# An encoder layer in split fp32 on one core: first stage's order, one running sum P1 + P6, operands a pair ahead, and the order at the norm, the stage change and the end

## The chip, the core and the metric

The kernel runs on one core of a Trainium2 chip. The core has a matrix engine (TensorE, in the profile PE, with its weight loads as PEld), a vector engine (VectorE, DVE), a scalar engine (ScalarE, ACT), a general engine (GpSimd, POOL), and a queue for DMA issues (SyncE, SP). Each engine takes its instructions in program order, and semaphores order them across engines. The metric is the device time of one execution in microseconds; the time of a kernel is the median over its runs.

## The reference

One layer of a streaming encoder over 1024 prompt frames and 32 frames of a running stream (1056 columns here), width 1024:

```
h   = rmsnorm(x)
P   = h @ w_in                    # GLU, q, k, v, gates: 10240 columns
A   = pointwise(swish(layernorm(depthwise_conv31(GLU(P)))))
B   = (swish(gate) * groupnorm(retention(q, k, v))) @ w_ret_out    # 4 heads, chunks
x   = x + (sigmoid(g_conv) * A + sigmoid(g_ret) * B) @ w_out
x   = x + relu(rmsnorm(x) @ w_mlp1)^2 @ w_mlp2                     # 1024 -> 4096 -> 1024
y   = rmsnorm(x)
```

The outputs are y for both streams and the new convolution and retention states. All inputs and outputs are float32.

## The kernel before

Features lie on the 128 partitions and frames in the free dimension. An operand of a matmul is split in two fp32r parts, a high one (a cast, mostly on ACT) and a low one (the rest, a subtraction on DVE or POOL). A product is three matmuls per slice of 128 inputs: high by high, high by low, low by high.

**First stage.** The products with `w_in`, `w_ro`, `w_co` and `w_o` are a list of jobs, one per 128 output features. `run` takes them in order: each job has three chunks of 352 frames, and `group` issues the 24 matmuls of one chunk (8 slices by 3) into one PSUM bank. `load` and `split` fetch a job's weight and split it ahead of use (`whi` on ACT; `wlo` on POOL, or DVE where `j.eng` says so, L110). Side work is written as Python generators: `run` advances each of `sides` by one step after every group, and those in `mids` also in the middle of a group. So the order on the engines is fixed by the program, with the steps of the side work dealt out over the groups: the first norm (`norm1`), the convolution's taps on DVE (`conv_side`, L374, 31 taps per channel tile), and a retention head (`retention`), whose step has the values transposed and split (`vtlo`, L425), the scores (`att`, `atlo`), the output `po` with its statistics, and the transposition back (`pto`, L500). `gated0` splits the gated retention output for the product with `w_ro`.

**First MLP product.** It is done in a Strassen manner, with seven products of sums of blocks instead of eight, by a table that gives for each step the functions to call (`at`, `c0`, `c1`, ...). `early` and `ss` are buffers for hidden units; L1092 copies one PSUM bank out into `early`. Hidden units are squared on ACT and spilled to memory (`usp`).

**Second MLP product.** Four groups of hidden units, each with seven products P1 to P7 in the order 1, 2, 6, 7, 4, 5, 3. A unit is half of such a product's weights, fourteen per group, and has four products of 12 matmuls of 264 columns. P2, P4 and P3 accumulate on the banks of P1, P7 and P5, so the earlier one's bank is read out (`evac`) before the later one starts on it. P1 + P6 is kept in `acc`, a part of the buffer `yy`, and is added to two or more blocks of the result `R` (`add_a`, L1260, on POOL, each time 128 x 528). `last_pair` loads the first two operands and weights of this stage during the last products of the first MLP product: both operands go through `yy`, the weights A11 into `raw` and A12 into `early`. All loads are issued on SP, in the program's order.

**End.** In the last group, squares of the finished rows are summed in `ss` (`sq_half`, `sq`); `begin(q)` makes the statistics of a quarter (`st_fn`, then the power on POOL), `spread(q)` broadcasts them (`bc_fn`), `out_row` scales a row and `store` writes it. The last unit is four products of quarters.

Of the kernel before, what the change touches and what calls it, by code (L numbers as in the profile page):

```python
# [10 lines left out]
ALU = mybir.AluOpType  # L11
# [48 lines left out]
def encoder_step(ctx: ExitStack, tc: tile.TileContext, xT, par_d, idn_d, cst_d, rot_d, w_in, w_co, w_ro,  # L60
# [63 lines left out]
    room = {}  # L124
# [16 lines left out]
    def group(n, c):  # L141
        j = jobs[n]
        xh, xl = (a[c] for a in j.rhs())
        ps = room.pop((n, c), None)
        if ps is None:
            ps = bank(f"ps{n}_{c}", xh.shape[-1])
        for k in range(KT):
            if k == KT // 2:
                advance(mids)
            for m, (a, x) in enumerate(((j.hi, xh), (j.hi, xl), (j.lo, xh))):  # L150
                nc.tensor.matmul(ps, lhsT=a[:, k, :], rhs=x[:, k, :],  # L151
                                 start=(k == 0 and m == 0), stop=(k == KT - 1 and m == 2))
# [13 lines left out]
    def run(count, order=None):  # L166

        n0 = pos[0]
        order = order or [(i, c) for i in range(count) for c in range(NCH)]
        left = [sum(i == j for j, _ in order) for i in range(count)]  # L170
        low = None
        for i, c in order:
            now = n0 + next(q for q in range(count) if left[q])
            if now != low:
                low = now
                load(low)
                split(low)
                load(low + 1)
                load(low + 2)
                split(low + 1)  # L180
            group(n0 + i, c)
            left[i] -= 1
            advance(sides)
        pos[0] = n0 + count
# [72 lines left out]
    with tc.manual_schedule():  # L257
        xv = xT.rearrange("k p t -> p k t")
        with ExitStack() as ph:
# [307 lines left out]
            def norm1():  # L567
                r0 = stat(0, enter(0))
                yield
                q = enter(1)  # L570
                yield
                yield
                next(r0)
                yield
                yield
                r1 = stat(1, q)
                scale(0, r0)
                turn(0)
                yield
                q = enter(2)  # L580
                yield
                yield
                next(r1)
                yield
# [34 lines left out]
            sides.append(conv_side())  # L619
# [3 lines left out]
            for h in range(H):  # L623
# [9 lines left out]
                sides.append(r)  # L633
# [12 lines left out]
            def gated0():  # L646
                for _ in range(4):
                    yield
                for c in range(NCH):
                    for p in range(2):  # L650
                        g0[p].append(actA.tile([P, KT, CW], F32R, tag=("hi", "lo")[p] + str(c), name=f"g0_{p}{c}"))
                    for k in range(0, KT, 2):
                        ks = slice(k, k + 2)
                        split_act(g0[0][c][:, ks, :], g0[1][c][:, ks, :], g0raw[:, ks, cs[c]])
                        if c == 0:
                            yield
                    yield
                    if c == 1:
                        yield
# [190 lines left out]
        def product(ps, w, x, fresh=True):  # L850

            for k in range(QW):
                for m, (a, b) in enumerate(((w[0], x[0]), (w[0], x[1]), (w[1], x[0]))):
# [28 lines left out]
        s1w = yy[:, 2 * KT * P:2 * KT * P + QW * P].rearrange("p (k f) -> p k f", k=QW)  # L882
# [85 lines left out]
        def mlp1(cc):  # L968
# [73 lines left out]
            def c19():  # L1042
                nc.scalar.copy(xop["T3"][0], blk[1, 2])
                nc.scalar.copy(wop["S4"][0], raws[1][0][:, QW:])

            def c21():
# [3 lines left out]
            def c23():  # L1050
                low("T4", blk[2, 1])
                prep_op(1, "A22")

            def c24():
                U = place(0)
                for i, src in enumerate((early[:, 0], ss[:, hs[0]], ss[:, hs[1]], early[:, 1])):
                    nc.scalar.activation(out=U[:, i], in_=src, func=AF.Square)

            for i, fn in ((0, c0), (1, c1), (2, c2), (5, c5), (8, c8),
                          (9, lambda: nc.scalar.copy(xop["T1"][0], blk[1, 1])), (10, c10), (14, c14),  # L1060
                          (15, lambda: prep_a(2)), (17, c17), (19, c19), (20, c24), (21, c21),
                          (23, c23), (24, lambda: sums(0, place(0))), (26, lambda: prep_s(2, 1)),
# [134 lines left out]
        def last_pair(e):  # L1197

            at(e - 3, lambda: load_xs(0, kpieces(yy)))

            def a():
                for hf in range(2):
                    load_quad(wp, "raw", 2, 0, "A11", hf)
                for hf in range(2):
# [3 lines left out]
            at(e, a)  # L1208
            for k in range(4):
                at(e + 2 + k, lambda k=k: cut_x(0, k))  # L1210
                at(e + 10 + k, lambda k=k: cut_x(1, k))
            at(e + 5, lambda: load_xs(1, kpieces(yy)))
# [7 lines left out]
        def mlp2(cd):  # L1220
# [37 lines left out]
            def add_a(f, i, half):  # L1258
                r = R[:, f, hs[half]]
                nc.gpsimd.tensor_tensor(out=r, in0=r, in1=acc[:, i, :], op=ALU.add)  # L1260

            def evac(g, p, i, ps):
                final = g == NG - 1
                if p == 1:
                    nc.scalar.copy(fold(acc[:, i, :]), two(ps))
                elif p == 2:
                    add(i, 0, ps)
                elif p == 6:
                    tt(out=fold(acc[:, i, :]), in0=two(ps), in1=fold(acc[:, i, :]), op=ALU.add)  # L1269
                    if final:  # L1270
                        add_a(i, i, 1)
                elif p == 7:
                    add(i + 4, 1, ps)
                elif p == 4:
                    add(i + 4, 0, ps)
                    if final:
                        add_a(i + 4, i, 0)
                        add_a(i + 4, i, 1)
                    else:
                        add_a(i, i, 1)  # L1280
                elif p == 5:
                    add(i + 4, 1, ps)
                else:
                    add(i, 1, ps)
                    if not final:
# [26 lines left out]
            def begin(q):  # L1312
                rs[q] = rstd_bc(ss[:, qs[q]], pn, ("pn", "pn"), ss[:, qs[q]], RMS_EPS, f"fn{q}")
# [80 lines left out]
            for gi, (i, s) in enumerate([(2, 0), (3, 0), (2, 1), (3, 1)]):  # L1394
                ps = banks[5, i][:, s, :ST]
                w = [a[:, 4 * (i % 2):4 * (i % 2) + 4] for a in units[nu - 1]]
                product(ps, w, x_of(len(xj) - 1, s), False)
                if gi == 0:
                    sq_half(7, 1, False)
                elif gi == 2:  # L1400
                    begin(2)
# [7 lines left out]
                elif gi == 2:  # L1409
                    spread(2)  # L1410
                    for f in PRE1:
                        out_row(f, qs[2], None, True)
                    store(4, 7, qs[2])

            for f in (7, 0):
                out_row(f, qs[2], bcs[2])
            begin(3)
# [142 lines left out]
```

## Time and profile before

| | |
|---|---|
| runs | 2236.2 us median of 3 (2234.68 to 2237.6) |
| profiled execution | 2240.53 us, its span 2238.8 us |
| mean granted clock of TensorE | 0.99 |
| busy: PE / DVE / POOL / ACT | 2172.7 / 1487.8 / 846.4 / 682.0 us |
| matmuls | 14850 |
| first stage, by the trace | 0 to about 1530 us |
| first MLP product | about 1530 to 1867 us |
| second MLP product and end | about 1867 to 2238.8 us |

In the rows of the profile a time is in us unless ns is said; `out<-in` names the tiles by the program's names, `x4` is a count, and `[0.88 <-DVE vtlo L425]` behind a row is the time that the engine stood idle before it and what released it. A row of waits has the total, the number and the longest. A row of windows has, for one stretch, its length, the busy time and count of PE, PEld, DVE, ACT and POOL, the granted clock of TensorE, the busy share of the DMA engines and GB/s. A row of the chain of waits has the start, the length and what the chain went through.

### The profile page before, as it was taken

The page shows a single profiled execution, that of the slowest core. Times are in us where ns is not written, and L with a number is a line of the kernel's source. Part 1 is how long each engine was busy: PE and PEld are TensorE (multiplying, and loading weights), DVE is VectorE, ACT ScalarE, POOL GpSimd, SP SyncE. Part 2 cuts the span into 40 slices and gives each one's busy share as a digit, 9 for nine tenths or more (in the row PEclk, how much of TensorE's full clock was granted, in tenths as well). Part 3 has the DMA queues.
Part 4 walks back from the last instruction along what each step waited for, and adds up shares of the span by engine and source line. Part 5 has one row for each costly group of instructions (what it writes and reads, how often), then busy time and mean ns, then how long its engine had stood idle before and what let it go on. Part 6 is the DMA issues. An engine that isn't in the chain of part 4 may idle for free.

```text
span 2238.8 us, 35237 instructions
## 1 busy us (share of the span) xinstructions
PE 2172.7 (97%) x14850; PEld 2125.3 (95%) x14850; DVE 1487.8 (66%) x1936; ACT 682.0 (30%) x1056; POOL 846.4 (38%) x553
## 2 busy tenths in 40 slices
PE   7999999999999999999999999999899999999996
PEld 6999999999999999999999999999899999999996
DVE  7948886178861889538753674458555446887886
ACT  4113211132111321113243232234443444343342
POOL 4635555355553566525520353101222222311324
PEclk9999999999999999999999999999999999999997
DMA  4112131111221113111442333342344438633422
GB/s 167 48 49 68 39 106 67 38 59 48 105 67 39 63 44 112 51 49 58 154 142 96 112 103 106 130 154 90 139 169 173 154 118 306 230 130 123 173 76 78
DMA packets 93679, 237.00 MB, mean 106 GB/s; under 512 B 11473, under 2 KB 30161, under 8 KB 89937
## 3 DMA queue, kind: packets, MB, share of 16 engines
q1 hardware_dynamic: 93520, 234.75, 30.3%
q8 instruction: 116, 1.90, 0.3%
q14 instruction: 43, 0.34, 0.0%
HBM read 165.40 MB, written 69.32 MB: 105 GB/s over the span
## 4 chain that ended last, share of the span: by engine, by line
PE 80%; DVE 12%; issue 3%; ACT 1%; DMA 1%; POOL 1%; SPq 0%; POOLq 0%; DVEq 0%; ACTq 0%
PE ps L151 47%; PE m L854 13%; PE d L854 12%; DVE yc L374 4%; PE po L406 3%; PE pkv L406 2%; DVE xB_lo L859 1%; DVE o L315 1%; PE pto L500 1%; DVE h_lo L224 1%; DMA raw<-w_in 1%; DVE ss L808 1%; POOL wlo L110 1%; DVE R L926 1%; PE pt L422 1%
## 5 line engine op out<-in xcount | busy, mean ns | idle before, releaser
L151 PE MATMUL ps<-h_hi,whi 128*128 128x352 f32 x1904 | 621.4, 326 | 9.5 <-ACT h_hi L223 7.9
L151 PE MATMUL ps<-h_hi,wlo 128*128 128x352 f32 x1904 | 616.2, 324 | 4.5 <-POOL wlo L110 3.8
L151 PE MATMUL ps<-h_lo,whi 128*128 128x352 f32 x1904 | 614.1, 323 | 1.1 <-DVE h_lo L224 1.1
L374 DVE SCALAR_TENSOR_TENSOR yc<-glu,par,yc 128x1086 f32<-128x1086 f32 x240 | 421.2, 1755 | 3.4
L151 PEld LDWEIGHTS ps<-h_hi,whi 128*128 128x128 f32 x1904 | 359.1, 189 | 13.4 <-ACT h_hi L223 7.9
L151 PEld LDWEIGHTS ps<-h_hi,wlo 128*128 128x128 f32 x1904 | 359.9, 189 | 6.5 <-POOL wlo L110 5.5
L151 PEld LDWEIGHTS ps<-h_lo,whi 128*128 128x128 f32 x1904 | 360.6, 189 | 4.0 <-DVE h_lo L224 2.6
L110 POOL TENSOR_TENSOR wlo<-raw,whi 128x1024 fp32r<-128x1024 f32 x80 | 232.2, 2903 | 192.6 <-ACT whi L109 192.6
L854 PE MATMUL d<-xB_hi,v_hi 128*128 128x264 f32 x840 | 241.0, 287 | 10.0 <-ACT yy L807 4.4
L854 PE MATMUL d<-xB_hi,v_lo 128*128 128x264 f32 x840 | 239.9, 286 | 0.8 <-DVE v_lo L859 0.8
L854 PE MATMUL d<-xB_lo,v_hi 128*128 128x264 f32 x840 | 239.6, 285 | 0.0
L109 ACT CAST whi<-raw 128x1024 fp32r<-128x1024 f32 x120 | 125.5, 1045 | 342.7 <-PE ps L151 235.1
L854 PEld LDWEIGHTS d<-xB_hi,v_hi 128*128 128x128 f32 x840 | 159.1, 189 | 11.2 <-ACT yy L807 4.6
L1260 POOL TENSOR_TENSOR R<-R,yy 128x528 f32<-128x528 f32 x48 | 78.0, 1642 | 222.4 <-DVE yy L1269 105.8
L854 PEld LDWEIGHTS d<-xB_hi,v_lo 128*128 128x128 f32 x840 | 159.3, 190 | 1.4 <-DVE v_lo L859 1.4
L854 PEld LDWEIGHTS d<-xB_lo,v_hi 128*128 128x128 f32 x840 | 159.3, 190 | 0.0
L991 POOL TENSOR_TENSOR R<-R 128x1056 f32<-128x1056 f32 x16 | 39.4, 2463 | 254.2 <-ACT R L1150 200.2
L1140 DVE TENSOR_TENSOR R<-m,R 128x528 f32<-128x528 f32 x73 | 51.6, 707 | 124.3 <-PE m L854 124.3
L293 DVE TENSOR_TENSOR qkv<-ps,rms 128x352 f32<-128x352 f32 x48 | 25.1, 523 | 129.0 <-PE ps L151 129.0
L312 POOL TENSOR_TENSOR gsig<-gsig,o 128x352 f32<-128x352 f32 x48 | 74.5, 1553 | 82.5 <-ACT gsig L311 82.5
L151 PE MATMUL ps<-g,whi 128*128 128x352 f32 x384 | 92.0, 323 | 2.5 <-DVE gsig L310 2.5
L151 PE MATMUL ps<-z,whi 128*128 128x352 f32 x384 | 91.5, 321 | 0.0
(288 smaller groups left out, 4948.5 us busy)
## 6 DMA issues: line engine op xcount, KB each, us to landing
raw<-w_in SPq DMA_DIRECT2D x80, 512.0 KB, 4.0
usp<-R SPq DMA_DIRECT2D x16, 2112.0 KB, 7.4
xs<-usp SPq DMA_DIRECT2D x26, 1056.0 KB, 5.0
A<-w SPq DMA_DIRECT2D x30, 512.0 KB, 6.9
gate<-gt SPq DMA_DIRECT2D x16, 528.0 KB, 3.0
gsp<-o SPq DMA_DIRECT2D x16, 528.0 KB, 3.0
raw<-w_ro SPq DMA_DIRECT2D x16, 512.0 KB, 3.8
raw<-w_o SPq DMA_DIRECT2D x16, 512.0 KB, 3.6
```

The costliest lines, as they stand in the source:

```text
L109: nc.scalar.copy(j.hi, j.raw)
L110: j.eng.tensor_tensor(out=j.lo, in0=j.raw, in1=j.hi.bitcast(F32), op=ALU.subtract)
L151: nc.tensor.matmul(ps, lhsT=a[:, k, :], rhs=x[:, k, :], start=(k == 0 and m == 0), stop=(k == KT - 1 and m == 2))
L224: nc.vector.scalar_tensor_tensor(out=lo, in0=src, scalar=pcol(gcol), in1=hi.bitcast(F32), op0=ALU.mult, op1=ALU.subtract)
L293: nc.vector.tensor_tensor(out=late["qkv"][:, 4 + e, cs[c]], in0=ps, in1=rms[:, cs[c]], op=ALU.mult)
L312: nc.gpsimd.tensor_tensor(out=t, in0=t, in1=o[:, e, cs[c]], op=ALU.mult)
L374: nc.vector.scalar_tensor_tensor(out=y, in0=glu[:, t:t + YL], scalar=w, in1=y, op0=ALU.mult, op1=ALU.add)
L406: nc.tensor.matmul(out, lhsT=w, rhs=x, start=start and i == 0, stop=stop and i == 2)
L854: nc.tensor.matmul(ps, lhsT=a[:, k, :], rhs=b[k], start=(fresh and k == 0 and m == 0), stop=(k == QW - 1 and m == 2), skip_group_check=not ...
L991: gt(out=U[:, 4:6], in0=U[:, 1:3], in1=U[:, 0:2], op=ALU.subtract)
L1140: tt(out=fold(u[i]), in0=two(ps), in1=fold(x), op=ALU.add)
L1260: nc.gpsimd.tensor_tensor(out=r, in0=r, in1=acc[:, i, :], op=ALU.add)
```

## The change

- **Weight order**: `group` issues, for the first chunk of each weight but the very first, all products with the high half before those with the low half (8 x 2, then 8).
- **Taps**: `conv_side` becomes two generators, each with at most one tap per step. One stands ahead of the retention head in `sides`, the other behind.
- **First norm**: the steps of `norm1` are dealt out in another order (third chunk's split sooner, first broadcast later).
- **gated0**: the second chunk's splits are dealt out two and two.
- **First MLP product**: the squares of the first hidden units (`square0`) and some splits stand at other steps.
- **Stage change**: both first operands are loaded twelve steps ahead, one into `yy` and one into `early`; A12 goes into `early` nine steps later than before.
- **P1 + P6**: `acc` is summed over all four groups, and added to `R` in the last group alone, now on DVE. P1 of groups 1 to 3 is added from PSUM on DVE, where ACT copied it.
- **End**: the statistics of the third quarter are issued in the middle of the last product, their broadcast behind it, and the POOL rows behind that.

```
-        for k in range(KT):
-            if k == KT // 2:
+        todo = [(k, m) for k in range(KT) for m in range(3)]
+        if n and c in (0, first_of.get(n, 0)):
+            todo.sort(key=lambda t: t[1] == 2)
+        for i, (k, m) in enumerate(todo):
+            if i == len(todo) // 2:
                 advance(mids)
...
-            def conv_side():
+            def conv_side(every):
...
-                    for _ in range(2 if n % 3 else 1):
-                        if conv_ops:
-                            conv_ops.pop(0)()
+                    if conv_ops and (every or n % 3):
+                        conv_ops.pop(0)()
...
-            sides.append(conv_side())
+            taps2 = conv_side(False)
+            sides.extend([conv_side(True), taps2])
...
-                sides.append(r)
+                sides.insert(sides.index(taps2), r)
...
-                    yield
-                    if c == 1:
+                        elif c == 1 and k == 2:
+
+                            yield
+                            yield
+                    if c == 0:
                         yield
...
-            at(e - 3, lambda: load_xs(0, kpieces(yy)))
+            def first():
+                load_xs(0, kpieces(yy))
+                load_xs(1, kpieces(late["early"]))
+            at(e - 12, first)
...
-                at(e + 10 + k, lambda k=k: cut_x(1, k))
-            at(e + 5, lambda: load_xs(1, kpieces(yy)))
+                at(e + 6 + k, lambda k=k: cut_x(1, k))
...
+            at(e + 9, a12)
...
-                nc.gpsimd.tensor_tensor(out=r, in0=r, in1=acc[:, i, :], op=ALU.add)
+                tt(out=r, in0=r, in1=acc[:, i, :], op=ALU.add)
...
-                if p == 1:
+                if p == 1 and g == 0:
                     nc.scalar.copy(fold(acc[:, i, :]), two(ps))
-                elif p == 2:
-                    add(i, 0, ps)
-                elif p == 6:
+                elif p in (1, 6):
                     tt(out=fold(acc[:, i, :]), in0=two(ps), in1=fold(acc[:, i, :]), op=ALU.add)
...
-                product(ps, w, x_of(len(xj) - 1, s), False)
+                product(ps, w, x_of(len(xj) - 1, s), False, (lambda: begin(2)) if gi == 3 else None)
...
-                elif gi == 2:
-                    begin(2)
+                elif gi == 3:
+                    spread(2)
...
-            for f in (7, 0):
-                out_row(f, qs[2], bcs[2])
-            begin(3)
+            for f in PRE1:
+                out_row(f, qs[2], None, True)
+            store(4, 7, qs[2])
+
+            begin(3, True)
+            for f in (7, 0):
+                out_row(f, qs[2], bcs[2])
+            next(rs[3])
```

What the change does to the order shows at three places. The first is DVE in a retention step of the first head: `gt` is an evacuation of a gate, `yc<-glu` a tap, `vtlo` the split of the transposed values, `att` and `atlo` the scores. Before (line numbers are each kernel's own, so 374 before is 380 now):

```order
L393 TENSOR_TENSOR gt_1553<-ps_1_1591,rms 128x352
L374 SCALAR_TENSOR_TENSOR yc_1489<-glu_1376,par,yc_1489 128x1086 x2
L425 TENSOR_TENSOR vtlo<-pt,vthi 128x512
L435 SCALAR_TENSOR_TENSOR ktlo<-pk,cst,kthi 128x256
L438 TENSOR_TENSOR att<-pk,cst 128x128
L442 TENSOR_TENSOR atlo<-att,athi 128x128
L393 TENSOR_TENSOR gt_1553<-ps_2_1650,rms 128x352
```

Now:

```order
L399 TENSOR_TENSOR gt_1553<-ps_1_1591,rms 128x352
L380 SCALAR_TENSOR_TENSOR yc_1489<-glu_1376,par,yc_1489 128x1086
L431 TENSOR_TENSOR vtlo<-pt,vthi 128x512
L441 SCALAR_TENSOR_TENSOR ktlo<-pk,cst,kthi 128x256
L444 TENSOR_TENSOR att<-pk,cst 128x128
L448 TENSOR_TENSOR atlo<-att,athi 128x128
L380 SCALAR_TENSOR_TENSOR yc_1489<-glu_1376,par,yc_1489 128x1086
L399 TENSOR_TENSOR gt_1553<-ps_2_1650,rms 128x352
```

Of the two taps ahead of `vtlo` one stands behind `atlo` now, ahead of the next evacuation.

The second place is ACT in the first MLP product, where a bank is copied out into `early`. `xT_hi` and `xB_hi` are casts for products that come later, `R<-early` and `R<-ss` the squares of the first hidden units. Before:

```order
L1070 ACTIVATE ss<-m_14303 128x528
L1043 CAST xT_hi<-R 128x2112
L1044 CAST xB_hi<-raw_13930 128x512
L1057 ACTIVATE R<-early 128x528
L1057 ACTIVATE R<-ss 128x528 x2
L1057 ACTIVATE R<-early 128x528
L1092 COPY early<-m_14358 128x528
```

Now:

```order
L1080 ACTIVATE ss<-m_14303 128x528
L1102 COPY early<-m_14357 128x528
L1058 ACTIVATE R<-early 128x528
L1062 CAST xT_hi<-R 128x2112
L1058 ACTIVATE R<-ss 128x528 x2
L1064 CAST xB_hi<-raw_13930 128x512
```

The copy stands right behind the relu into `ss`; both casts and three of the squares follow it, and the first square stands ahead of these rows.

The third place is DVE in the last group of the second MLP product, at the evacuation of P4 (`R<-d`). `xB_lo` and `v_lo` are splits of the next operand and weights, `ss<-ss,yy` sums squares, and `R<-R,yy` is the sum P1 + P6 added to a block. Before:

```order
L1256 TENSOR_TENSOR R<-d_0_20461,R 128x528
L859 TENSOR_TENSOR xB_lo<-xs,xB_hi 128x528 x2
L808 TENSOR_TENSOR ss<-ss,yy 128x528
L1256 TENSOR_TENSOR R<-d_1_20493,R 128x528
L859 TENSOR_TENSOR xB_lo<-xs,xB_hi 128x528
L859 TENSOR_TENSOR v_lo<-A_31_19890,v_hi 128x1024
```

Now:

```order
L1271 TENSOR_TENSOR R<-d_0_20425,R 128x528
L1275 TENSOR_TENSOR R<-R,yy 128x528 x2
L871 TENSOR_TENSOR xB_lo<-xs,xB_hi 128x528 x2
L818 TENSOR_TENSOR ss<-ss,yy 128x528
L1271 TENSOR_TENSOR R<-d_1_20457,R 128x528
L1275 TENSOR_TENSOR R<-R,yy 128x528 x2
L871 TENSOR_TENSOR xB_lo<-xs,xB_hi 128x528
L871 TENSOR_TENSOR v_lo<-A_31_19862,v_hi 128x1024
```

Two adds of the sum follow each such evacuation on DVE; before, POOL had all of them, 48 in the four groups.

More of the change, by code (lines that the diff above doesn't have):

```diff
@@ L123, in encoder_step @@
     held, deferred, normed = [], [], [0]
-    room = {}
+    room, first_of = {}, {}
     rings = [(pm, "pm")]
@@ L146, in group @@
             ps = bank(f"ps{n}_{c}", xh.shape[-1])
-        for k in range(KT):
-            if k == KT // 2:
+        kinds = [(j.hi, xh), (j.hi, xl), (j.lo, xh)]
+        todo = [(k, m) for k in range(KT) for m in range(3)]
[3 more added lines that the diff above has]
+            if i == len(todo) // 2:
                 advance(mids)
-            for m, (a, x) in enumerate(((j.hi, xh), (j.hi, xl), (j.lo, xh))):
-                nc.tensor.matmul(ps, lhsT=a[:, k, :], rhs=x[:, k, :],
-                                 start=(k == 0 and m == 0), stop=(k == KT - 1 and m == 2))
+            a, x = kinds[m]
+            nc.tensor.matmul(ps, lhsT=a[:, k, :], rhs=x[:, k, :], start=(i == 0), stop=(i == len(todo) - 1))
         old = len(deferred)
@@ L169, in run @@
         order = order or [(i, c) for i in range(count) for c in range(NCH)]
+        for i, c in reversed(order):
+            first_of[n0 + i] = c
         left = [sum(i == j for j, _ in order) for i in range(count)]
@@ L576, in norm1 @@
                 r1 = stat(1, q)
-                scale(0, r0)
-                turn(0)
                 yield
@@ L581, in norm1 @@
                 yield
+                scale(0, r0)
                 yield
                 next(r1)
+                turn(0)
                 yield
@@ L848, in tick, with product @@
             step[0] += 1
-        def product(ps, w, x, fresh=True):
+        def product(ps, w, x, fresh=True, mid=None):
             for k in range(QW):
+                if mid and k == QW // 2:
+                    mid()
                 for m, (a, b) in enumerate(((w[0], x[0]), (w[0], x[1]), (w[1], x[0]))):
@@ L1040, in c17, with square0, c22 @@
                 nc.scalar.copy(xop["T4"][0], blk[2, 1])
-            def c19():
+            def square0(*rows):
+                U = place(0)
+                src = (early[:, 0], ss[:, hs[0]], ss[:, hs[1]], early[:, 1])
+                for i in rows:
+                    nc.scalar.activation(out=U[:, i], in_=src[i], func=AF.Square)
+            def c22():
+                square0(3)
                 nc.scalar.copy(xop["T3"][0], blk[1, 2])
+                square0(1, 2)
                 nc.scalar.copy(wop["S4"][0], raws[1][0][:, QW:])
-            def c21():
                 low("T3", blk[1, 2])
                 tt(out=wop["S4"][1], in0=raws[1][0][:, QW:], in1=wop["S4"][0].bitcast(F32), op=ALU.subtract)
[L1050 to L1057, printed above, removed]
             for i, fn in ((0, c0), (1, c1), (2, c2), (5, c5), (8, c8),
                           (9, lambda: nc.scalar.copy(xop["T1"][0], blk[1, 1])), (10, c10), (14, c14),
-                          (15, lambda: prep_a(2)), (17, c17), (19, c19), (20, c24), (21, c21),
-                          (23, c23), (24, lambda: sums(0, place(0))), (26, lambda: prep_s(2, 1)),
+                          (15, lambda: prep_a(2)), (16, lambda: square0(0)), (17, c17),
+                          (20, lambda: low("T4", blk[2, 1])), (22, c22), (23, lambda: prep_op(1, "A22")), (24, lambda: sums(0, place(0))), (26, lambda: prep_s(2, 1)),
                           (26, lambda: prep_s(2, 3)), (27, lambda: prep_s(2, 2)), (28, lambda: prep_op(2, "S2")),
@@ L1203, in a, with a12 @@
                     load_quad(wp, "raw", 2, 0, "A11", hf)
+            at(e, a)
+            for k in range(4):
+                at(e + 2 + k, lambda k=k: cut_x(0, k))
+                at(e + 6 + k, lambda k=k: cut_x(1, k))
+            def a12():
                 for hf in range(2):
```

35 lines of the change are left out of this document (9 added, 26 removed).

## The prediction, made before the changed kernel was run

> **What bounds the kernel now.** I read the page first (busy times, then groups), then the waits of TensorE, then the granted clock in short windows around the longest waits, and last the rows of the engine that each wait names.
>
> ```profile
> PE 2172.7 (97%) x14850; PEld 2125.3 (95%) x14850; DVE 1487.8 (66%) x1936; ACT 682.0 (30%) x1056; POOL 846.4 (38%) x553
> L1260 POOL TENSOR_TENSOR R<-R,yy 128x528 f32<-128x528 f32 x48 | 78.0, 1642 | 222.4 <-DVE yy L1269 105.8
> ...
> PE pto L500 <- DVE vtlo L425: 8.1, 8, 1.2
> PE m L854 <- ACT early L1092: 6.3, 2, 5.6
> PE bc_n L218 <- DVE rms L214: 4.5, 3, 2.7
> PE d L854 <- ACT yy L807: 4.4, 1, 4.4
> PE ps L151 <- POOL wlo L110: 3.8, 6, 0.7
> PE d L854 <- DVE R L1140: 2.9, 1, 2.9
> PE ps L151 <- DVE wlo L110: 2.6, 3, 1.0
> PE ps L151 <- DVE gsig L310: 2.5, 1, 2.5
> ```
>
> TensorE is the bound: 2172.7 of 2238.8 us busy. The change leaves its number of matmuls as it is, so it can save only idle time (66.1 us in all) and matmuls that ran at a low clock. The waits (total, times, longest) say which idle time. The low clock shows in these windows (length; busy time and count of PE, PEld, DVE, ACT, POOL; granted clock):
>
> ```profile
> 27.50:30.00 2.50, 2.50 (x15) 2.50 (x15) 2.36 (x4) 1.74 (x2) 0.00 (x0) 0.72 0.03 7
> 30.00:32.50 2.50, 2.50 (x12) 2.50 (x11) 1.25 (x3) 1.18 (x3) 0.60 (x1) 0.60 0.00 0
> 1512.50:1515.00 2.50, 2.50 (x16) 2.50 (x16) 1.93 (x4) 1.14 (x3) 0.00 (x0) 0.68 0.48 182
> 1515.00:1517.50 2.50, 2.50 (x16) 2.50 (x15) 1.90 (x4) 1.31 (x3) 0.00 (x0) 0.64 0.10 34
> 1572.50:1575.00 2.50, 0.97 (x4) 0.97 (x5) 2.50 (x3) 1.48 (x3) 0.00 (x0) 0.50 0.00 0
> 1575.00:1577.50 2.50, 2.50 (x14) 2.50 (x13) 1.09 (x1) 0.00 (x0) 1.26 (x1) 0.50 0.00 0
> 1577.50:1580.00 2.50, 2.50 (x19) 2.50 (x19) 0.00 (x0) 0.81 (x2) 2.42 (x2) 0.85 0.00 0
> 1920.00:2160.00 240.00, 240.00 (x1979) 240.00 (x1978) 195.67 (x219) 95.87 (x139) 57.10 (x37) 1.00 0.41 143
> 2192.50:2195.00 2.50, 1.60 (x7) 1.63 (x8) 2.08 (x4) 2.20 (x4) 0.00 (x0) 0.53 0.00 0
> 2195.00:2197.50 2.50, 2.50 (x13) 2.50 (x12) 1.08 (x1) 2.47 (x4) 0.00 (x0) 0.50 0.00 0
> 2197.50:2200.00 2.50, 2.50 (x15) 2.50 (x15) 1.57 (x4) 0.39 (x2) 0.00 (x0) 0.61 0.00 0
> ```
>
> Busy time times (1 - clock) is what each episode costs: 2.5 x (0.28 + 0.40) = 1.7 us after the norm's 2.7 us wait; 2.5 x (0.32 + 0.36) = 1.7 after the gap at 1510; 0.49 + 1.25 + 0.37 = 2.1 after the 5.6 us wait; 0.75 + 1.25 + 0.98 = 3.0 after the 4.4 us wait. Removing such a wait is worth the wait and its episode. The row of 1920 to 2160 is the undisturbed pace: 240.00 / 1979 = 0.121 us for a matmul of 264 columns, so 1.45 for a product of 12 and, by the columns, 0.16 us for a matmul of 352.
>
> **The change part by part.**
>
> *First norm.* The first broadcast goes half a group later, so the wait of 2.7 us and its 1.7 us leave that place. But the third chunk's h_lo now stands ahead of the gate's evacuations on DVE, and DVE has work for most of this stretch:
>
> ```profile
> 20.00:48.00 28.00, 24.36 (x147) 23.31 (x146) 24.07 (x35) 8.95 (x15) 14.18 (x11) 0.94 0.27 99
> ```
>
> DVE 24.07 of 28 us leaves 3.9 us: the next two broadcasts hang on the same sums, so I book -0.5 only, between -2 and +1.5.
>
> *Retention.* One convolution tap moves from ahead of vtlo to behind atlo; the number of taps is the same.
>
> ```profile
> 209.94 4.69 DVE L374 SCALAR_TENSOR_TENSOR yc<-glu,par,yc 128x1086 f32<-128x1086 f32 x2
> 214.55 0.68 DVE L425 TENSOR_TENSOR vtlo<-pt,vthi 128x512 fp32r<-128x512 f32 x1
> ...
> 215.28 0.66 PE L500 MATMUL pto<-ident,on 128*128 128x128 f32 x4 [0.88 <-DVE vtlo L425]
> ```
>
> Here two taps take 4.69 us, vtlo follows at once and TensorE waits 0.88. One tap fewer brings vtlo 4.69 / 2 = 2.3 us forward; the longest of the eight waits is 1.2. So all 8.1 could go; I take -7.5. Bounds: -8.1, and -4 if the tap behind atlo makes the statistics late instead.
>
> *Weight order.* For a weight's first chunk the products with its low half come last, so that half is needed 16 matmuls later: 16 x 0.16 = 2.6 us, or 1.9 at 264 columns, while the longest wait on wlo is 1.0. The six POOL waits (3.8) and one of the three DVE waits (0.7, at 1120) should go: -3.5 of 4.5, since the evacuations then come due earlier on a DVE that has the taps to do; bounds -4.5 and -1.5. The other two DVE waits, 0.95 each, lie at the w_out product, ahead of the low clock of 1512.5. I book -3.0 of 1.9 + 1.7 (1.6 for the waits, 1.4 for the clock), since other waits remain there that can keep the clock low; bounds -4.2 and -0.5.
>
> *Gated product.* Four splits stand ahead of an evacuation for which TensorE waits 2.5:
>
> ```profile
> 1144.30 3.88 DVE L229 TENSOR_TENSOR g<-g0raw,g 128x704 fp32r<-128x704 f32 x4
> 1148.11 0.51 DVE L310 TENSOR_TENSOR gsig<-ps,rms 128x352 f32<-128x352 f32 x1
> ```
>
> Two of them move behind it: 3.88 / 2 = 1.9 us sooner, -1.9 (bounds -2.5, -0.5).
>
> *Order in the first MLP product.* TensorE waits 5.6 us for the copy of a bank, which on ACT stands behind two casts and four squares:
>
> ```profile
> 1568.39 0.60 ACT L1070 ACTIVATE ss<-m 128x528 f32<-128x528 f32 x1
> 1568.89 1.94 ACT L1043 CAST xT_hi<-R 128x2112 fp32r<-128x2112 f32 x1
> ...
> 1573.40 0.58 ACT L1092 COPY early<-m 128x528 f32<-128x528 f32 x1
> ```
>
> It now comes right behind the relu of 1568.39, at about 1569.0, 4.4 us sooner. The wait falls to 1.2 and the 2.1 us of low clock go: -6.5, of which I take -6.0. The 4.4 us of casts and squares are not saved, they come behind the copy; if they are late for the next product, -3 is left. The good end is the whole wait and episode, -7.7.
>
> *Operands a pair ahead.* The chain of waits at the stage change:
>
> ```profile
> 1867.65 10.39 DMA yy<-usp
> ...
> 1878.72 0.04 DVE xB_lo L859
> ...
> 1879.35 0.71 DVE R L1140
> ```
>
> The second operand's load waited for yy, took 10.39 us, and DVE's evacuation stood behind the split that needs it. Now it lands in `early`, twelve products sooner, and 2.9 us of wait go. In return A12 goes to `early` only after that split, nine products on: the SP queue waits there with the R reloads, A21, A22 and the third operand behind it. A wait at the second weight unit could cost as much again: -2.4, bounds -2.9 and +2.5.
>
> *P1 + P6 in one sum.* 48 adds on POOL (78.0 us) go, and 12 ACT copies; DVE gets 12 adds from PSUM (0.70 in the row of 2192.56 below) and, in the last group, 12 adds of the sum. From 1920 to 2160 TensorE never waits, so nothing is saved there: 0, at worst +8 (12 waits of 0.7). In the last group POOL's adds stretch DVE's operations whose inputs both lie in SBUF:
>
> ```profile
> 2180.99 1.21 DVE L859 TENSOR_TENSOR v_lo<-s,v_hi 128x1024 fp32r<-128x1024 f32 x1
> 2188.60 2.32 DVE L859 TENSOR_TENSOR v_lo<-A,v_hi 128x1024 fp32r<-128x1024 f32 x1
> 2192.56 0.70 DVE L1256 TENSOR_TENSOR R<-d,R 128x528 f32<-128x528 f32 x1
> ...
> 2188.20 3.87 POOL L1260 TENSOR_TENSOR R<-R,yy 128x528 f32<-128x528 f32 x2 [1.84 <-DVE R L1256]
> ```
>
> Beside a POOL add v_lo takes 2.32 instead of 1.21, 1.1 more; the add from PSUM keeps its 0.70. The last group has twelve POOL adds (the last two in the POOL row), which at 1.1 each stretch DVE by up to 13 us; I count 12. The new adds, with none on POOL beside them, cost 12 x 0.62 = 7.4 (0.70 with an overlap of 0.08 between neighbours), so DVE is 4.6 us ahead at the evacuation of 2192.56, for which TensorE waits 4.4 (the view names ACT; the bank is freed by that row). Wait and episode, 4.4 + 3.0, go.
>
> *End.* The last product no longer stands behind the third statistics:
>
> ```profile
> 2218.31 0.84 PE st_fn L205 x6
> ...
> 2222.22 2.85 PE d L854 x12
> ...
> 2226.66 1.43 PE st_fn L205 x6
> ```
>
> Before, the product waits from the statistics (2218.31) to the end of their broadcast (2222.22) and the last statistics hang on the product: 2226.66. Now those statistics run in its middle, so it is over before their broadcast, and the last statistics hang on that broadcast's end, some 1 us past 2222.22 since the statistics start half a product later: near 2223.2, which is 3.5 us sooner. Three POOL rows now stand ahead of the last power; they end about when its input is there. Last group and end: 4.4 + 3.0 + 3.5 = 10.9, of which I take -10; bounds -12 and -5.5 (part of the stall stays).
>
> Sum: -0.5 - 7.5 - 3.5 - 3.0 - 1.9 - 6.0 - 2.4 - 10 = -34.8. The profiled execution took 2240.53 (span 2238.8 and 1.7 around it), 4.3 above the median of 2236.2; it would be 2205.7, and the median 2201.4.
>
> [...]
>
> **The rivals.**
>
> *Half comes back.* DVE is the next bound: without the waits on wlo and vtlo TensorE ends its groups sooner, and their evacuations come due sooner than DVE can take them. For it: DVE 24.07 of 28 in the first norm. Against: it is 66% busy overall. Half the sum: 2218.8.
>
> *Retention and weight order do nothing.* The tap taken away behind vtlo delays the statistics of the same step, and the wait moves from vtlo to them; wlo's waits become evacuation waits. Without 7.5 and 3.5: 2212.4.
>
> *P1's evacuation on DVE stops TensorE.* In groups 1 to 3 the second product's bank is the first's, and it starts two products (2.9 us) after the first ends. Where ACT evacuated, DVE now must, behind splits of 1.2 and 0.7. Twelve such places: from 2.9 us of wait at each on, the whole gain is gone; at 3.3 us, with the low clock behind some, it is 2201.4 + 39.6 = 2241. Against it: in the row of 1920 to 2160 DVE already evacuates the other shared banks at the same distance and TensorE has no gap. For it: there DVE is busy 195.67 of 240 us, 82%, and 12 x 0.70 = 8.4 come on top.
>
> **How the numbers follow.** Forecast 0.60; half back 0.15; no first-stage gain 0.10; all bounds at their good ends (2193 and below) 0.04; P1's evacuation 0.11, of which 0.05 within 0.2% (about 4.5 us, what a measurement of this kernel can tell) and 0.06 beyond. That is 0.89 faster, 0.05 the same, 0.06 slower. The range 2190 to 2221 holds the forecast with its bounds and both smaller gains; only the last rival and the tails lie outside.
>
> **What would show it.** The vtlo row gone from TensorE's waits; no wait over 1.5 us between 1560 and 1880; no clock under 0.9 at 1510 to 1520 and 1570 to 1580; DVE's v_lo near 1.21 in the last group and the 4.4 us wait gone; the last statistics 3 to 4 us nearer to the last product. Wrong it is if TensorE waits for yy in groups 1 to 3, for v_hi out of `early`, or for the third chunk of the norm by more than 3 us.

## The result, and the profile of the changed kernel

The changed kernel takes 2214.5 us (median of four runs, 2211.1 to 2215.7) against 2236.9 for the kernel before beside it (2234.7 to 2238.6): a ratio of 0.990, 95% interval 0.988 to 0.991. It is 22.4 us faster; 34.8 were forecast. The time lies inside the range of 2190 to 2221. The profiled execution of the change took 2215.39, that of before 2240.53, so the two profiles differ by 25.1 us, and the accounts below are of that difference.

The page's busy times, and the shares of its chain that ended last:

```profile
PE 2167.9 (98%) x14850; PEld 2126.1 (96%) x14850; DVE 1465.0 (66%) x1960; ACT 678.1 (31%) x1044; POOL 789.4 (36%) x505
PE 87%; DVE 7%; issue 2%; ACT 1%; DMA 1%; POOL 1%; POOLq 0%; DVEq 0%; ACTq 0%
```

TensorE is still the bound, with the same 14850 matmuls. Its idle time fell from 66.1 to 45.7 us. What it waits for now (total, times, longest):

```profile
PE ps L156 <- ACT h_hi L229: 6.6, 1, 6.6
PE bc_n L224 <- DVE rms L220: 4.1, 5, 1.8
PE bc_fn L224 <- DVE ss L220: 3.5, 2, 1.8
PE ps L156 <- ACT whi L109: 2.8, 2, 1.7
PE ps L156 <- DVE qkv L285: 2.3, 2, 1.9
PE d L866 <- ACT yy L817: 2.1, 1, 2.1
PE m L866 <- ACT R L1145: 2.0, 1, 2.0
PE m L866 <- ACT early L1102: 1.8, 2, 1.1
PE st_n L211 <- DVE rms L557: 1.7, 2, 0.9
```

The first row is the first load of the program. vtlo and wlo are gone, `early` fell from 6.3 to 1.8, yy from 4.4 to 2.1. Three rows took their place: `whi` 2.8 (1.0 before), the evacuation of q, k and v on DVE, `qkv` 2.3 (1.1 before), and a wait for `R L1145` in the first MLP product.

Both kernels issue the same number of matmuls, so the time can be laid out by the start of the k-th one. This table is worked out from the starts in the two traces (us; the last row ends with the last matmul):

```
matmuls        what lies there               before   after   moved   forecast
0-300          first load, first norm         70.26   68.46    -1.8     -0.5
300-6600       w_in and retention           1039.51 1029.72    -9.8    -11.0
6600-6960      gated product                  61.96   59.03    -2.9     -1.9
6960-8950      w_ro, w_co                    302.18  304.76    +2.6      0
8950-9420      w_out and its norm             63.49   62.57    -0.9     -3.0
9420-9900      first MLP product, start       67.10   61.50    -5.6     -6.0
9900-12050     first MLP product, rest       261.50  265.26    +3.8      0
12050-12420    stage change                   50.02   46.60    -3.4     -2.4
12420-14400    second product, to group 2    240.35  240.35     0.0      0
14400-end      last group, end                74.78   67.76    -7.0    -10.0
```

Of the first row 1.25 is the first load, which ended earlier in this execution (the first matmul starts at 6.65 instead of 7.89); the norm itself is worth about nothing, since a second profile of before has 60.8 for the stretch behind that load, and the variants have 61 to 62.7.

Two rows were not foreseen at all. In the first, TensorE has no idle time in either kernel, and yet the same work takes longer. The stretch from matmul 6960 to 8950, of before:

```profile
1171.73:1473.91 302.18, 302.18 (x1993) 301.55 (x1992) 155.24 (x249) 92.71 (x165) 79.33 (x75) 1.00 0.36 116
```

and of the change (length; busy time and count of PE, PEld, DVE, ACT, POOL; clock; DMA share; GB/s):

```profile
1157.21:1461.97 304.76, 304.76 (x1992) 304.12 (x1992) 156.29 (x250) 92.70 (x165) 79.40 (x75) 1.00 0.36 116
```

Full clock, PE busy from end to end, the same other work beside it, and 2.6 us more. I call this the pace.

The second is a transfer to memory in the middle of the first MLP product. The chain there, in order of time:

```profile
1587.08 1.20 DVE xB_lo L871
...
1588.29 8.62 DMA usp<-R
...
1597.01 0.61 ACT R L1145
```

An evacuation by ACT into R must wait until R's old content has been written out; TensorE then waits 2.0 us for the bank, and its clock falls:

```profile
1597.50:1600.00 2.50, 2.34 (x15) 2.34 (x16) 0.71 (x1) 2.50 (x4) 0.00 (x0) 0.80 0.35 143
1600.00:1602.50 2.50, 2.50 (x14) 2.50 (x13) 0.00 (x0) 1.23 (x2) 1.45 (x1) 0.52 0.03 7
```

2.0 of wait and 0.47 + 1.20 = 1.7 of low clock make 3.7 of the 3.8 us of that row.

### The profile page after: what moved, and what is told of

It is laid out like the page before. It is cut to its first block, busy times and chain, and to the rows that moved or that the text cites. A ratio compares the mean times of both kernels' runs of the same rounds, so it can differ in the third digit from the quotient of the medians.

```text
span 2213.6 us, 35142 instructions
## 1 busy us (share of the span) xinstructions
PE 2167.9 (98%) x14850; PEld 2126.1 (96%) x14850; DVE 1465.0 (66%) x1960; ACT 678.1 (31%) x1044; POOL 789.4 (36%) x505
## 4 chain that ended last, share of the span: by engine, by line
PE 87%; DVE 7%; issue 2%; ACT 1%; DMA 1%; POOL 1%; POOLq 0%; DVEq 0%; ACTq 0%
PE ps L156 54%; PE m L866 12%; PE d L866 12%; PE po L412 3%; PE pkv L412 2%; DMA usp<-R 1%; DVE xB_lo L871 1%; PE pt L428 1%; PE pto L506 1%; PE pk L436 1%; DVE yc L380 1%; DVE R L938 1%; DVE ss L818 0%; DVE o L321 0%; PE pk L434 0%
## 5 line engine op out<-in xcount | busy, mean ns | idle before, releaser
L156 PE MATMUL ps<-h_hi,wlo 128*128 128x352 f32 x1904 | 527.6, 324 | 0.0
L380 DVE SCALAR_TENSOR_TENSOR yc<-glu,par,yc 128x1086 f32<-128x1086 f32 x240 | 410.2, 1709 | 2.0
L156 PEld LDWEIGHTS ps<-h_hi,wlo 128*128 128x128 f32 x1904 | 343.4, 188 | 0.0
L299 DVE TENSOR_TENSOR qkv<-ps,rms 128x352 f32<-128x352 f32 x48 | 25.1, 523 | 129.6 <-PE ps L156 129.6
L416 POOL TENSOR_TENSOR slo<-s,shi 128x1024 fp32r<-128x1024 f32 x28 | 76.4, 2730 | 40.7 <-ACT shi L415 40.5
L870 ACT CAST v_hi<-A 128x1024 fp32r<-128x1024 f32 x44 | 46.3, 1052 | 139.9 <-PE d L866 97.1
```

Source lines behind the costliest of these rows:

```text
L156: nc.tensor.matmul(ps, lhsT=a[:, k, :], rhs=x[:, k, :], start=(i == 0), stop=(i == len(todo) - 1))
L299: nc.vector.tensor_tensor(out=late["qkv"][:, 4 + e, cs[c]], in0=ps, in1=rms[:, cs[c]], op=ALU.mult)
L380: nc.vector.scalar_tensor_tensor(out=y, in0=glu[:, t:t + YL], scalar=w, in1=y, op0=ALU.mult, op1=ALU.add)
L416: nc.gpsimd.tensor_tensor(out=s2[1], in0=s, in1=s2[0].bitcast(F32), op=ALU.subtract)
L870: nc.scalar.copy(w[0], src)
```

## The experiments

Theory 1 is that the weight order (high-half products first) makes all 352-column products slower, also where no group is sorted. Theory 2 is that the pace is the execution's and not the kernel's, and that the weight order is worth what was forecast. 

**The kernel before, again.**

> The kernel before once more, unchanged, for a second profile. In the two profiles at hand a 352-column matmul of the first stage follows the one before it after 159.5 ns (before) and 160.8 ns (after) on average, in groups whose order is the same too, which costs the change some 7 us. Theory 1: the pace belongs to the kernel (the sorted weight order slows TensorE); then it is 159.5 here again. Theory 2: it belongs to the run; then it may lie anywhere between 158.9 and 161.

2237.7. Its stretch from 6960 to 8950 has 302.18 once more, to the hundredth: the pace belongs to the kernel. Other stretches differ between the two profiles of before: the gated product takes 61.1 instead of 62.0, and w_out 63.1 instead of 63.5.

**Without the weight order.**

```
-        if n and c in (0, first_of.get(n, 0)):
-            todo.sort(key=lambda t: t[1] == 2)
```

> The changed kernel without the weight order (each group goes slice by slice as before). Theory 1 (the order slows TensorE by 1.2 ns per matmul): pace back at 159.5 ns, which gives 7 us, and the waits on wlo return, 4.5 us before 1160 and 1.9 at w_out: about 1 us faster than the changed kernel, 2213. Theory 2 (the pace is the run's): only the waits return: 4 to 6 us slower than the changed kernel, 2219 to 2221.

2211.1 (2209.9 to 2211.7), ratio 0.988 [0.987, 0.990]: 3.4 us faster than with it, where theory 2 wanted it slower. The two sets of runs just touch (the change's begin at 2211.1). The low halves are waited for again:

```profile
PE ps L154 <- POOL wlo L110: 3.7, 6, 0.7
PE ps L154 <- DVE wlo L110: 3.5, 5, 1.0
```

7.2 us of waits came back, less the 2.3 us that `whi` loses, and the whole is still shorter: from 300 to 6600 it takes 1027.8 us (1029.7 with the order), from 6960 to 8950 303.1 (304.8). The mean distance of two 352-column matmuls, from the starts in the traces, is 160.7 ns with the order and 159.5 without.

**The old tap order.** Both taps stand ahead of vtlo again, one generator as before.

> The changed kernel with the taps' old generator (one or two taps ahead of each retention step, none behind). My theory: the eight waits of the transposition on vtlo come back, 8 us, so 2222. Rival: the order of the taps only moves the wait; then within 2 us of the changed kernel, 2213 to 2217.

2223.4 (2221.7 to 2224.0), ratio 0.994 [0.992, 0.995]: 8.8 us slower than the change.

```profile
PE pto L506 <- DVE vtlo L431: 8.1, 8, 1.2
```

The row is back as it was, and from 300 to 6600 it takes 1041.6, 11.9 more. In this profile the clock also falls at 347 us, behind a wait of 1.9 us that the change has too without the fall, so up to 1.7 of the 11.9 may belong to this execution. The tap order is the largest single gain of the change.

**P1 + P6 as before.** POOL adds the sum group by group, ACT copies P1.

> The changed kernel with P1 + P6 as before (copied by ACT in each group, added to R on POOL in all four groups). My theory (DVE's lead at the end comes from the POOL adds being gone): DVE's v_lo beside a POOL add is at 2.3 us again, the stall in the last group is 4.4 us instead of 2.1 and its low clock 3.0 instead of 1.7, so 3.6 us slower, 2218. Rival (what DVE does in groups 1 to 3 costs nothing or gains, and the new adds in the last group eat the lead): within 1 us of the changed kernel. Until 2130 us no difference in either.

2216.2 (2215.3 to 2219.0), ratio 0.991 [0.989, 0.992]. In groups 0 to 2 nothing differs (240.35 from 12420 to 14400, to the hundredth); the last group and the end take 71.21 instead of 67.76.

```profile
PE d L866 <- ACT yy L817: 4.4, 1, 4.4
```

So P1's evacuation on DVE stops nothing, and the sum is worth 3.4 us there: 2.3 of the long wait and 1.1 of small ones. The two make up the whole difference of the stretch, so the low clock behind the long wait costs 1.7 us, as in the change. The medians are only 1.6 apart, for which the next run has a reason.

**The change, again.**

> The changed kernel once more, unchanged, for a second profile and for its time beside the next ones. The first profile has a wait of 2.0 us on the bank copied at L1145, behind a spill that took 8.6 us, and 1.7 us of low clock after it; the three profiles of variants, which have the same code there, have not. So: no such wait, the stretch from 1586 to 1851 us at 261.9 instead of 265.3. Pace of 352-column matmuls 160.8 ns again. Median 2212 to 2215.

2214.8, but its runs lie between 2212.0 and 2217.7. The pace is 160.7 ns again. The wait for the transfer is not there this time:

```profile
1586.69 8.31 DMA usp<-R
...
1595.10 0.61 ACT R L1145
1595.70 0.04 issue
1595.75 9.27 PE m L866 x74
```

The transfer starts 1.6 us earlier and takes 0.3 less. TensorE itself is only 0.25 us earlier there, so most of this lies in when the transfer is issued; what decides that isn't shown. ACT is done at 1595.7, and behind it TensorE runs at full clock:

```profile
1597.50:1600.00 2.50, 2.50 (x23) 2.50 (x23) 0.00 (x0) 2.09 (x3) 0.86 (x1) 1.00 0.04 10
```

From 9900 to 12050 it takes 262.1, not 265.3. The changed kernel reaches that place within some 2 us of the edge, and which side it falls on differs from execution to execution. Of the ten other kernels' profiles six have it near 261.7 and three at 265.2; one lies between, at 263.6, where TensorE waits 1.9 us and the clock stays up.

**A low half at most three steps late.** A product with the low half is put off by three steps of k instead of to the end, so that never many of one kind follow each other.

```
-            todo.sort(key=lambda t: t[1] == 2)
+            todo.sort(key=lambda t: (t[0] + 3 * (t[1] == 2), t[1]))
```

> The changed kernel with another order in the same groups: a slice's low-weight product comes three slices after its high ones, in turn with them, so that wlo is needed 8 matmuls (1.3 us) later than without the order, and no long run of one kind stands at the end but three. Theory A (the run of eight products of one kind sets TensorE on the slow pattern): pace at 159 to 159.6 ns and no wlo wait over 0.1: 2207 to 2208. Theory B (any break of the three-cycle does): pace at 160.8 ns, 2212 to 2215.

2210.9 (2208.5 to 2213.4), ratio 0.988 [0.987, 0.990]. The mean distance is 160.0 ns, between the two theories' figures; wlo is waited for 0.8 us in all. From 300 to 6600 it takes 1026.5, the least of all kernels.

**The stage change as before**, and **the first MLP product's squares as before.**

> The changed kernel with the stage change as before (both operands through yy, A12 at once). My theory: the wait of 2.9 us behind the 10 us load of yy comes back, and the wait on v_lo with it: 3.0 to 3.5 us slower, 2217. Rival (a wait only moved): within 1 us of the changed kernel.

> The changed kernel with the squares and splits of the first MLP product as before. My theory: the wait of 5.6 us on the copy into early and its 2.1 us of low clock return: 5.5 us slower in the stretch from 1524 to 1586, of which 0.4 comes back behind it: 2218 to 2220. Rival (the spill behind it is the bound, as the first profile's 2.0 us wait says): the gain is given back at the spill, 2 us slower at most, 2216.

Loads late: 2217.1 (2214.7 to 2219.4), ratio 0.991 [0.989, 0.992]; from 12050 to 12420 it takes 50.0 instead of 46.6, with the old row:

```profile
PE d L866 <- DVE R L1150: 2.8, 1, 2.8
```

Squares first: 2216.5 (2216.0 to 2219.6), ratio 0.991 [0.989, 0.992]; from 9420 to 9900 it takes 66.5 instead of 61.5:

```profile
PE m L866 <- ACT early L1104: 6.3, 2, 5.6
```

Each stretch gives back most of what the step had brought there (3.4 of 3.4, and 5.0 of 5.6), but the medians only 2.5 and 2.0. For the squares the rival was right in the time, and the one trace has a likely reason: behind its long wait that kernel meets the transfer late enough (261.50 from 9900 to 12050, no wait), so it keeps the 3.4 us that the changed kernel loses in some executions.

**One sorted group.** What does the order do to the rhythm? Here the first group of weight 92 alone is sorted (at 1274 to 1278 us). Theory A said that one sorted group slows all that follow up to the next break of TensorE's stream, theory B that only the sorted group and its neighbours, a group or two, are slow.

```
-        if n and c in (0, first_of.get(n, 0)):
+        if n == 92 and c == 0:
```

> The changed kernel with the weight order in one single group, the first chunk of weight 92 (in the product with w_ro, near 1210 us; no other group has it). Theory A (TensorE keeps a rhythm over the groups, and the sorted group throws it into a slower one that lasts): the 352-column pace is 159.2 ns before that group and near 160.9 behind it, up to the next break in the stream. Theory B (the cost lies in the sorted groups and their neighbours): 159.0 before and, a group or two later, behind. Time 2211 by B, 2212 by A.

2213.0 (one run). The distances of the starts in the trace, in ns, repeat every six matmuls:

```
before the sorted group       161 155 159 161 162 156     mean 159.0
behind it                     164 162 164 159 158 159     mean 161.0
means of the groups behind it 161.1 161.5 161.1 160.3 158.9
```

One sorted group throws the rhythm into a slower one, which lasts for about four groups (some 15 us) and then comes back by itself. A is right that it outlasts the group, and wrong on its end; B is right that it ends by itself, and has the end too soon. With a sorted group at every third group the stretch is slower in every row. Times for 199 matmuls each, from 6960 on (us):

```
before      31.62 31.69 31.36 31.43 31.59 31.40 31.62 31.62
change      32.02 32.01 31.63 31.55 31.81 31.68 32.02 32.02
no order    32.49 31.79 31.36 31.43 31.59 31.40 31.62 31.62
one group   31.62 31.69 31.36 31.44 31.74 31.40 31.62 31.62
```

The kernel without the order starts this stretch with a wait of 0.4 us for a low half; here too the slow rhythm behind it lasts one or two rows and is gone. Why the one rhythm is slower isn't shown by anything here.

**Sorted where it pays, adds later.** The low half is put off by three steps where wlo was waited for, nowhere in w_ro and w_co; and the eight adds of the sum behind P4's evacuations in the last group stand behind P7's.

```
-        if n and c in (0, first_of.get(n, 0)):
-            todo.sort(key=lambda t: t[1] == 2)
+        if n and (n < 80 or n >= 104) and c in (0, first_of.get(n, 0)):
+            todo.sort(key=lambda t: (t[0] + 3 * (t[1] == 2), t[1]))
...
-                    if final and p == 4:
+                    if final and p == 7:
```

> The changed kernel with three slices' delay instead of the full order, and only where weights were waited for (w_in and w_out; w_ro and w_co go slice by slice), and with the sums' eight adds of P4 put behind P7, one unit sooner, where DVE twice stands idle for 0.45 us. Theory (a lead is kept only from DVE's last idle moment on): the stall of 2.1 us in the last group falls by those 0.9 us to 1.2, 0.9 us less at the end, and up to 1.7 more if the clock then stays up; if the lead from earlier counted too, the eight adds (5.0 us) moved ahead would end the stall. Pace in w_ro and w_co 159.0 ns. Time: 2208 to 2210, against 2214.7 of the changed kernel.

2204.9 (2204.2 to 2207.3), ratio 0.986 [0.984, 0.987]: the fastest, 9.6 us under the change and 32 under before. I had expected 2208 to 2210. The last group's wait, and the window that holds it:

```profile
2162.64 0.36 PE L866 MATMUL d<-xB_hi,v_hi 128*128 128x264 f32 x1 [0.54 <-ACT yy L817]
```

```profile
2162.50:2165.00 2.50, 2.36 (x19) 2.39 (x20) 1.33 (x2) 2.44 (x5) 0.00 (x0) 1.00 0.00 0
```

The wait fell by 1.6 us, not 0.9, and at 0.5 the clock stays up, so the low clock went with it: 65.4 us for the last group and the end, where the change has 67.8. The two profiles differ by 10.0 us: 4.0 in the first stage, 3.6 at the transfer, for which this execution does not wait, and 2.4 here. The 3.6 can't be booked for the two edits, since the change's second profile does not wait there either.

**The end as before**, all else as in the change.

> The changed kernel with the end's order as before (statistics of the third quarter and their broadcast ahead of the last product). My theory: the last product waits 4 us for them again, and the last statistics hang on it: 3.5 us slower, 2218. Rival (the three POOL rows now ahead of the last power give the gain back): within 1 us of the changed kernel, 2215.

2214.3 (2212.1 to 2214.7), ratio 0.989 [0.988, 0.991]: no difference. My theory of 2218 falls. The rival had the time, though by POOL rows that stand in the way, and these end at 2202.7, before the last power starts at 2203.3. What happened is in the rows of TensorE. The change:

```profile
2195.55 0.83 PE L211 MATMUL st_fn<-ones,ss 128*128 128x1 f32 x6
...
2199.03 0.81 PE L224 MATMUL bc_fn<-ss,ones 128*128 128x128 f32 x6 [1.81 <-DVE ss L220]
2201.51 1.41 PE L211 MATMUL st_fn<-ones,ss 128*128 128x1 f32 x6 [1.67 <-DVE ss L818]
2204.58 1.42 PE L224 MATMUL bc_fn<-ss,ones 128*128 128x128 f32 x6 [1.66 <-DVE ss L220]
```

With the old end:

```profile
2194.96 0.83 PE L211 MATMUL st_fn<-ones,ss 128*128 128x1 f32 x6 [0.59 <-DVE ss L818]
2197.45 0.81 PE L224 MATMUL bc_fn<-ss,ones 128*128 128x128 f32 x6 [1.66 <-DVE ss L220]
...
2201.43 0.80 PE L211 MATMUL st_fn<-ones,ss 128*128 128x1 f32 x6 [1.61 <-DVE ss L818]
2203.89 1.42 PE L224 MATMUL bc_fn<-ss,ones 128*128 128x128 f32 x6 [1.66 <-DVE ss L220]
```

With the old end the clock is at 1.00 from 2195 to 2200, where the broadcast takes 0.81 us and the product behind it 1.7 (2198.11 to 2199.81), and both orders have their last statistics at 2201.5. In the change the clock has fallen before those statistics (0.50 from 2200 to 2205; they take 1.41 us instead of 0.80), so from there to the last broadcast it takes 3.07 us, with the old end 2.46. In all eleven profiles with the new end the clock has fallen before those statistics; the old end beside the other edits has this one profile.

**No weight order, adds later**, to part the two edits of the fastest kernel.

> The changed kernel without any weight order, and with P4's eight adds put behind P7. It tells what the delayed order in w_in and w_out is worth on top. Theory (the order only moves waits: what wlo gives back in waits, it loses in pace and in the waits on whi): within 2 us of the version with the delay of three slices, 2205 to 2207. Rival (the waits of 4.5 us on wlo in w_in are real and the delayed order removes them): 2208 to 2209. In the last group the stall is 0.5 us in both and the clock stays up.

2209.7 (2207.0 to 2211.7), ratio 0.987 [0.986, 0.989]. Its last group and end take 65.1 us, as in the fastest kernel, so that gain belongs to the adds. Most of the rest is the low halves:

```profile
PE ps L154 <- POOL wlo L110: 6.1, 7, 2.1
...
PE ps L154 <- DVE wlo L110: 3.2, 4, 1.0
```

It is 4.8 us above the fastest, with runs that just touch (2204.2 to 2207.3 and 2207.0 to 2211.7). The theory wanted 2 us at most, so the rival is nearer. Of the 4.8 us between the two profiles 2.0 lie at the transfer (263.64 against 261.68) and 3.2 in the first stage; a small loss at the end goes the other way. Putting the low half off by three steps is likely worth some 3 us, but less sure than the rest.

## Why the prediction was right or wrong, step by step

*First norm* (-0.5): about nothing; the booked half microsecond is below what the profiles tell apart.

*Retention* (-7.5): right. The eight waits went, and taking the step back costs 8.8 us.

*Weight order* (-3.5 in w_in and retention, -3.0 at w_out): **this step failed.** Its working counted the waits on wlo and took the duration of a matmul as fixed. The waits on wlo in w_in did go, though at one place (343 us) into a wait of 1.9 us for the evacuation `qkv`. But the pace took more: in 300 to 6600 the distances of two starts that are over 170 ns in either trace, and so hold the waits, shrank by 14.1 us and the stretch by 9.8, so 4.3 went into the pace; 2.6 more went in w_ro and w_co, where nothing had been waiting. At w_out the wait changed its name. The casts of ACT in the change:

```profile
1497.48 0.42 ACT L817 ACTIVATE sq<-R 128x264 f32<-128x264 f32 x1 [2.47 <-DVE R L831]
1497.81 1.03 ACT L109 CAST whi<-raw 128x1024 fp32r<-128x1024 f32 x1
```

and the matmul that needs it:

```profile
1498.89 0.39 PE L156 MATMUL ps<-m_mh,whi 128*128 128x264 f32 x1 [1.73 <-ACT whi L109]
```

whi's cast stands on ACT behind a square that waits for an evacuation of DVE. Waits were 1.9 (wlo) and 0.5 (whi) before and are 2.8 (whi) now. The stretch is 0.9 us shorter than in the profile of before, and 0.5 than in its second one, which had no low clock there. So the 1.4 us that were booked for the clock were hardly there to be had. The change's second profile shows it too. It has the low clock again:

```profile
1500.00:1502.50 2.50, 2.50 (x15) 2.50 (x14) 2.00 (x4) 0.83 (x3) 0.00 (x0) 0.54 0.53 198
1502.50:1505.00 2.50, 2.50 (x18) 2.50 (x18) 1.93 (x5) 1.32 (x4) 0.00 (x0) 0.78 0.16 54
```

That is 1.7 us, and yet the stretch takes the same 62.57: the second wait on `whi` (1.05 us) is gone, and a later one is shorter. A slow TensorE lost there what it would have waited for ACT and DVE.

Instead of -6.5 the whole step is worth +3.4 by the medians of the change and the kernel without it, and +2.8 by their stretches up to w_out.

*Gated product* (-1.9): right, -2.9 (-2.0 against the second profile of before).

*Order in the first MLP product* (-6.0): right in its place, -5.6. What the prediction did not follow is who is early next: TensorE now reaches the bank that the transfer of R holds up about 5 us sooner, and in some executions pays 3.4 to 3.8 us there.

*Operands a pair ahead* (-2.4): right, -3.4. The wait at the second weight unit that bounded it did not come.

*P1 + P6 in one sum* (0): right to the hundredth in groups 0 to 2.

*Last group and end* (-10): direction right, -7.0 (the stall 2.3, its low clock 1.2, small waits of DVE's evacuations 1.0, the end 2.5). Two terms were mis-sized. The stall was to vanish, since DVE was reckoned 4.6 us ahead: twelve stretched operations against twelve adds, 12 - 7.4. But DVE had still been idle in that stretch of before:

```profile
2167.97 0.71 DVE L1256 TENSOR_TENSOR R<-d,R 128x528 f32<-128x528 f32 x1 [0.38 <-PE d L854]
```

Time that is saved ahead of this idle moment only makes it longer. Behind it lie 8.3 us of the stretch, against the 5.2 us of adds that stand behind the same point of the change, which gives about 3; measured, the wait fell by 2.3, from 4.4 to 2.1. The account is of the right size and not exact: for the moved adds it gave 0.9, and 1.6 were measured. The rows of DVE and TensorE in the change:

```profile
2169.25 1.22 DVE L871 TENSOR_TENSOR v_lo<-A,v_hi 128x1024 fp32r<-128x1024 f32 x1
2170.39 0.70 DVE L818 TENSOR_TENSOR ss<-ss,yy 128x528 f32<-128x528 f32 x1
2171.00 0.70 DVE L1271 TENSOR_TENSOR R<-d,R 128x528 f32<-128x528 f32 x1
```

```profile
2171.85 0.36 PE L866 MATMUL d<-xB_hi,v_hi 128*128 128x264 f32 x1 [2.12 <-ACT yy L817]
```

v_lo takes 1.22 without a POOL add beside it, as foreseen, yet it is late. And behind these 2.1 us the clock falls:

```profile
2172.50:2175.00 2.50, 2.50 (x14) 2.50 (x13) 0.81 (x3) 2.47 (x5) 0.00 (x0) 0.50 0.00 0
2175.00:2177.50 2.50, 2.50 (x19) 2.50 (x19) 2.34 (x4) 1.24 (x3) 0.08 (x1) 0.83 0.00 0
```

1.25 + 0.43 = 1.7 of the 3.0 stay. That isn't sure either: with the same 2.1 us the clock fell in six profiles and stayed up in three. Of one of these, the kernel with the old tap order:

```profile
2181.05 0.36 PE L865 MATMUL d<-xB_hi,v_hi 128*128 128x264 f32 x1 [2.13 <-ACT yy L816]
2182.50:2185.00 2.50, 2.50 (x23) 2.50 (x23) 0.99 (x1) 2.47 (x4) 0.00 (x0) 1.00 0.00 0
```

Its last group and end take 67.0 us, not 67.8. The *End* (-3.5 of these 10) is worth 0.1 by its own run: it was reckoned from rows of before that had run at half clock, where the broadcast took 1.42 us and the product 2.98 (2222.08 to 2225.06), against 0.81 and 1.7 with the old end above. The end did become 2.5 us shorter, since the clock falls later: before, the third broadcast and the last product ran at half clock (0.50 from 2220 to 2225), and with the same order in the kernel above they did not (1.00 from 2195 to 2200).

Of the rivals, *retention and weight order do nothing* gives the nearest time (2212.4), and that is luck: it was right for the second only, and what retention brought was lost elsewhere. *Half comes back* (2218.8) was to happen on DVE's evacuations; some of it did, at `qkv`, but most came back in the pace and at one transfer. *P1's evacuation on DVE stops TensorE* did not happen.

## What to carry to other kernels

When TensorE never idles in a stretch, the order of its matmuls can itself be a cost (here 2.6 us in 302): compare the time of the same number of matmuls before and after. Time saved on an engine ahead of its last idle moment before the wait is mostly lost (here 4.6 us were reckoned with it and about 3 without it, and the wait fell by 2.3), and a row that was taken at half clock overstates what it costs at full clock (here 1.42 us for a broadcast, against 0.81). Where a wait is taken away, follow the engine to its next dependence, here a transfer that had been just in time.

## What the runs showed of the hardware

The pace was not expected: at full clock, with no wait, 352-column matmuls follow each other every 159.0 or 161.0 ns, in two rhythms of six. In the one run made for it, a sorted group threw them into the slower one for about 15 us. The stretch of 264 columns (240.35 us) was the same in all fourteen profiles.

The clock did not follow the length of a wait alone. Behind the 2.1 us in the last group it fell in six profiles (0.50 and 0.83 in the two windows of the change) and stayed up in three (1.00 with the old tap order). At the transfer it fell to 0.52 behind 2.0 us in the change, and stayed up behind 1.9 us in the kernel without the order and with later adds. Behind the 5.6 and the 4.4 us of the kernel before it fell to 0.50, and behind the 0.5 us of the fastest kernel it stayed at 1.00. So the same wait cost an episode in one execution and none in another; what decides it isn't shown.
